# Stick-breaking attention inside a hybrid decoder step: narrow tiles' sums a beat earlier, exponentials behind the newest split, masked weights split a beat later

## The chip, the cores and the metric

The kernel runs on one core of a Trainium2 chip. The time is the device time of one execution in microseconds (us). Engines are TensorE (PE in the profile; PEld is its weight load), VectorE (DVE), ScalarE (ACT), GpSimd (POOL) and SyncE (SP), which issues almost all DMAs here.

## The reference

One layer of a decoder step: an input projection of 1,072 tokens (16 learned, 1,024 of a prompt, 8 x 4 new ones of samples), eight heads of stick-breaking attention beside four heads of gated linear attention, SiLU gates and an output projection. The change lies in the attention of the prompt:

```python
def stick_break_weights(z, mask):
    sp = jnp.where(mask, jax.nn.softplus(z), 0.0)
    later = lax.cumsum(sp, axis=z.ndim - 1, reverse=True) - sp
    return jnp.where(mask, jnp.exp(jax.nn.log_sigmoid(z) - later), 0.0)

a = stick_break_weights(sb_logits(qb, k, bias), kpos[None, :] < qpos[:, None])
o = jnp.einsum('bhqk,bkhd->bqhd', a.astype(v.dtype), v)
```

A key's weight is its own sigmoid, times what all later keys have left of the stick: softplus of the logits is summed over the later keys, and the exponential of logit minus sum is the weight.

## The kernel before, in words

All float32 products are made from an upper part (rounded to the matmul's format) and a lower part (the rest), three matmuls for each product of two split operands. Attention runs in the stage from about 100 to 860 us. The main stream on TensorE is the in-projection (`inproj`, L347 to L349): head by head the columns of v, k and q, each as 16 steps of 128 rows in three chunks of tokens. After every six of these matmuls the program calls `W.beat()`. At a beat a small scheduler (`Weaver`) resumes generators, each of which writes some instructions and yields a number of beats to wait. So the order on every engine is laid down in beats, and each engine then works in that order; an engine that waits for an operand holds back all that stands behind it.

Per head there are 14 tiles (qi, j): query block qi (0: queries 16 to 527; 1: 528 to 1039) against a group j of 126 keys, from the last key group down. Keys lie on the partitions, queries on the columns. Query block 1 has tiles j = 8 to 0, block 0 j = 4 to 0. A tile that is cut by the causal border has fewer columns: 32, 158, 284 and 410 for (1,8) to (1,5), 24, 150, 276 and 402 for (0,4) to (0,1), and about 512 elsewhere. One tile (`attend_tile`) goes through these steps:

- z = k^T q, three matmuls (L599 to L601) into a PSUM bank `z`.
- X = softplus(z + bias): VectorE's minimum (L605), ScalarE's exponential and logarithm (L606, L607), VectorE's maximum (L608); GpSimd clears what lies above the border (L611).
- Two beats later, and when the next key group's tile has its sums: ScalarE copies that tile's total into row 0 of X (the carry, L617), and X is split: `hi_s` by ScalarE (L584), `lo_s` by VectorE (L585).
- D1 = 4 beats later the sums: two matmuls with a triangular matrix, `hi_s` and `lo_s`, onto z (L620, L621). z is now logit minus sum.
- Y = exp(z + bias) on ScalarE (L625), the border cleared by GpSimd (L627), Y split into `hi_a` and `lo_a` by the same function `split_tmp`.
- D2 = 6 beats later the product with V into `O`, three matmuls (L633 to L635).

Upper parts share three buffers (tag `hi`), lower parts three (`lo`), X and Y three. ScalarE also splits the k columns of the next head (L703), the weights (`wh_q`, `wh_v`, L187) and V (`V`, L576). V of a head is not taken from the projection directly: `load_v` clears a staging tile `vr` on GpSimd (L571), loads the head's values into it from the output tensor that they were stored to (DMAs L572 and L574), and splits it (L576 on ScalarE, L578 on VectorE), in three pieces.

Three more generators run beside this: `z_feed` (the decode samples' logits on VectorE, L469, from page loads `kp`, L426, and query copies `qb`, L446), `weight_forms` (differences of the output weights, L496), and `level_masks` (seven masks for the gated linear attention, built on GpSimd from a cleared tile by pairs of selections, L404 to L408). `spread(ins)` and the note "behind" add a dependency that only orders: the instruction is placed later than another (for `spread`, the newest in-projection matmul, `W.mark`) in the program's order, and no semaphore is added for it.

Of the kernel before, what the change touches and what calls it, by code (L numbers as in the profile page):

```python
# [15 lines left out]
AF = mybir.ActivationFunctionType  # L16
ALU = mybir.AluOpType
# [37 lines left out]
NOSYNC = mybir.DependencyInfo(mybir.DependencyClass.NoSync, mybir.DependencyReason.DATA)  # L55
# [34 lines left out]
def hybrid_step(ctx: ExitStack, tc: tile.TileContext, x_prompt, x_sample, cache_k, cache_v, state_gla,  # L90
# [5 lines left out]
    vec, act, pool = nc.vector, nc.scalar, nc.gpsimd  # L96
# [19 lines left out]
    def stage(nm, dt=F32):  # L116
        return stg.tile([P, 384], dt, tag="stg", name=nm)
# [77 lines left out]
    with tc.tile_pool(name="xp", bufs=2) as xp, tc.tile_pool(name="xps", bufs=5, space=PSUM) as xps:  # L195
# [109 lines left out]
        for c, (lo, hi) in enumerate(XCHUNKS):  # L305
            n = hi - lo
            for k in range(NK):
# [10 lines left out]
                ins = act.activation(hh[k][:, lo:hi], ps[:, :n], AF.Copy, scale=gpre[:, k:k + 1]).ins  # L318
# [79 lines left out]
    def level_masks():  # L398

        for m in (64, 32, 16, 8, 4, 2, 1):  # L400
            nb = P // (2 * m)
            a = stage(f"lv{m}")[:, :P]
            av = a.rearrange("p (n two m) -> p n two m", two=2, m=m)
            pool.memset(a, 1.0)  # L404
            for two, k0 in ((1, 0), (0, m)):
                pool.affine_select(av[:, :, two, :], av[:, :, two, :], [[-2 * m, nb], [0, m]], ALU.is_ge, 0.0,
                                   base=-k0, channel_multiplier=1)
                pool.affine_select(av[:, :, two, :], av[:, :, two, :], [[2 * m, nb], [0, m]], ALU.is_ge, 0.0,  # L408
                                   base=k0 + m - 1, channel_multiplier=-1)
            lvl[m] = dk.tile([P, P], U8, tag=f"lvl{m}", bufs=1, name=f"lvl{m}")  # L410
            vec.tensor_copy(lvl[m][:], a)
            yield 16
# [66 lines left out]
    def spread(ins):  # L479

        if W.mark is not None:
            tc.add_manual_dep(ins.ins, W.mark.name, NOSYNC, reason="spread")
# [54 lines left out]
    with tc.tile_pool(name="sp", bufs=1) as sp, tc.tile_pool(name="sps", bufs=1, space=PSUM) as sps:  # L537
# [26 lines left out]
        def load_v(h, V, behind):  # L564

            for c in range(3):
                st = stage(f"vr{h}_{c}")
                sv = st[:].rearrange("p (a d) -> p a d", d=P)
                nt = 3 if c < 2 else 2
                src = new_v_prompt[0, 0, :, h, :]  # L570
                pool.memset(st[:], 0.0)  # L571
                nc.sync.dma_start(sv[1:KT + 1, :nt], src[c * 378:c * 378 + nt * KT].rearrange("(a p) d -> p a d", p=KT))  # L572
                if c == 2:
                    nc.sync.dma_start(sv[1:33, 2, :], src[8 * KT:REAL])  # L574
                vs = slice(3 * c, 3 * c + 3)
                ins = act.copy(V[0][:, vs, :], sv)  # L576
                tc.add_manual_dep(ins.ins, behind.name, NOSYNC, reason="behind")
                vec.tensor_tensor(V[1][:, vs, :], sv, V[0][:, vs, :].bitcast(F32), ALU.subtract)  # L578
                yield 1

        def split_tmp(X, rows, n, nm):
            a = sp.tile([P, 512], F32R, tag="hi", bufs=3, name=f"hi_{nm}")
            b = sp.tile([P, 512], F32R, tag="lo", bufs=3, name=f"lo_{nm}")
            act.copy(a[:rows, :n], X)  # L584
            vec.tensor_tensor(b[:rows, :n], X, a[:rows, :n].bitcast(F32), ALU.subtract)  # L585
            return a, b

        def attend_tile(h, qi, qlo, qhi, j, jmax, q, kt, V, carry, O):
            nm = f"{h}_{qi}_{j}"
            k0 = j * KT  # L590
            nk = P
            c0 = max(qlo, k0)
            col = c0 - qlo
            n = qhi - c0
            qs = slice(c0 - META, c0 - META + n)
            ks = slice(j * P, j * P + nk)
            z = sps.tile([P, 512], F32, tag="z", bufs=4, name=f"z{nm}")
            zz = z[:nk, :n]
            mm(zz, kt[0][:, ks], q[0][:, qs], start=True, stop=False)  # L599
            mm(zz, kt[0][:, ks], q[1][:, qs], start=False, stop=False)  # L600
            mm(zz, kt[1][:, ks], q[0][:, qs], start=False, stop=True)  # L601
            bias = bias0[:nk, h:h + 1]
            xt = sp.tile([P, 512], F32, tag="X", bufs=3, name=f"X{nm}")
            X = xt[:nk, :n]
            vec.tensor_scalar(X, zz, bias, 30.0, ALU.add, ALU.min)  # L605
            act.activation(X, X, AF.Exp)  # L606
            act.activation(X, X, AF.Ln, bias=1.0)  # L607
            vec.scalar_tensor_tensor(X, zz, bias, X, ALU.add, ALU.max)  # L608
            w = min(n, k0 + KT - c0)
            if w > 0:  # L610
                pool.affine_select(X[:, :w], X[:, :w], [[1, w]], ALU.is_gt, 0.0, base=c0 - k0 + 1, channel_multiplier=-1)  # L611
            yield 2
            if j < jmax:
                while carry.get(qi, (None,))[0] != j + 1:
                    yield 1
                _, cz, ccol = carry[qi]
                act.activation(X[0:1, ccol - col:], cz[0:1, :], AF.Copy, scale=-1.0)  # L617
            sh, sl = split_tmp(X, nk, n, "s" + nm)
            yield D1
            mm(zz, ntri0[:nk, :nk], sh[:nk, :n], start=False, stop=False, skip_group_check=True)  # L620
            mm(zz, ntri0[:nk, :nk], sl[:nk, :n], start=False, stop=True, skip_group_check=True)  # L621
            carry[qi] = (j, zz, col)
            yt = sp.tile([P, 512], F32, tag="X", bufs=3, name=f"Y{nm}")
            Y = yt[:nk, :n]
            act.activation(Y, zz, AF.Exp, bias=bias)  # L625
            if w > 0:
                pool.affine_select(Y[:, :w], Y[:, :w], [[1, w]], ALU.is_gt, 0.0, base=c0 - k0 + 1, channel_multiplier=-1)  # L627
            ah, al = split_tmp(Y, nk, n, "a" + nm)
            yield D2
            if j == jmax:  # L630
                O[qi] = sps.tile([P, 512], F32, tag="O", name=f"O{h}_{qi}")
            o = O[qi]
            mm(o[:, col:], V[0][:nk, j, :], ah[:nk, :n], start=(j == jmax), stop=False, skip_group_check=True)  # L633
            mm(o[:, col:], V[0][:nk, j, :], al[:nk, :n], start=False, stop=False, skip_group_check=True)
            mm(o[:, col:], V[1][:nk, j, :], ah[:nk, :n], start=False, stop=(j == 0), skip_group_check=True)  # L635
            if j == 0:
                st = sp.tile([P, 512], F32, tag="X", bufs=3, name=f"ost{h}_{qi}")
                act.copy(st[:], o[:])
                nc.sync.dma_start(od[h][:, qlo - META:qhi - META], st[:])
# [10 lines left out]
        D1, D2 = 4, 6  # L650
# [83 lines left out]
        W.spawn(z_feed(lambda n: 2), lasting=True)  # L734
        W.spawn(weight_forms(), 10, lasting=True)
        W.spawn(level_masks(), 30, lasting=True)
        for h in range(HEADS):
            if h == HEADS - 1:
# [977 lines left out]
```

## Time and profile before

| | us |
|---|---|
| median of three runs | 2051.52 (2050.90 to 2051.88) |
| profiled execution | 2053.43, span 2051.7 |
| granted TensorE clock, mean | 0.999 |
| TensorE busy | 2014.6 (98%) |
| VectorE busy | 1548.0 (75%) |
| ScalarE busy | 954.4 (47%) |
| GpSimd busy | 91.8 (4%) |

The profiled execution is one run under the hardware profiler; its own time stands beside the span of its records. Busy times are sums over the instructions of an engine. Timelines give an instruction's start, its length, its line, and, in brackets, how long the engine was idle before it and what ended that. Matmuls are pipelined, so that the lengths of two neighbours overlap; the distance between their starts is what a matmul costs.

### The profile page before, as it was taken

To read this page: it belongs to the slowest core of one execution; us is meant where nothing else is said; L and a number is where in the kernel's file an instruction comes from. 1 tells how busy PE (TensorE), PEld (TensorE's weight loads), DVE (VectorE), ACT (ScalarE), POOL (GpSimd) and SP (SyncE) were. 2 spreads that over 40 slices of the span, in tenths; PEclk is the share of its full clock that TensorE was granted. 3 is DMA by queue.
4 is the path that set the end of the run, shared out by engine and by line. 5 is a ranking of instruction groups with operands and counts; after the bars stand their busy time and mean duration, and the time that the engine had idled before them with its cause. 6 is when DMAs were issued, how large, how long until landed. Compare 5 with 4: busy or idle time off the path is not lost.

```text
span 2051.7 us, 41912 instructions
## 1 busy us (share of the span) xinstructions
PE 2014.6 (98%) x12443; PEld 1857.7 (91%) x12443; DVE 1548.0 (75%) x6282; ACT 954.4 (47%) x2297; POOL 91.8 (4%) x338
## 2 busy tenths in 40 slices
PE   6999999999999999999999999999999999999998
PEld 5999999999999998999999999999888897788776
DVE  7368989888988989999798898978444347453576
ACT  7355556564655556432534335353433325432342
POOL 0012000101000000100000000000000000000000
PEclk9999999999999999999999999999999999999999
DMA  6355454644555542443342433335767666352475
GB/s 203 100 137 151 143 155 135 170 132 143 150 164 145 141 129 76 130 114 84 98 117 78 127 83 108 101 88 166 247 226 236 215 227 195 131 164 73 138 266 200
DMA packets 371821, 301.85 MB, mean 147 GB/s; under 512 B 42360, under 2 KB 312104, under 8 KB 371592
## 3 DMA queue, kind: packets, MB, share of 16 engines
q1 hardware_dynamic: 371288, 298.64, 48.7%
q8 instruction: 98, 1.61, 0.3%
q14 instruction: 131, 1.07, 0.2%
q10 hardware_dynamic: 304, 0.53, 0.1%
HBM read 241.75 MB, written 57.31 MB: 146 GB/s over the span
## 4 chain that ended last, share of the span: by engine, by line
PE 80%; DVE 8%; DMA 5%; issue 3%; ACT 3%; SPq 1%; POOL 0%; DVEq 0%; ACTq 0%; POOLq 0%
PE acc_g L347 5%; PE acc_g L348 5%; PE acc_g L349 5%; PE b L1617 4%; PE b L1619 4%; PE b L1618 4%; PE acc_k L347 3%; PE acc_k L349 3%; PE acc_k L348 3%; PE acc_gv L347 3%; DVE jk L469 3%; PE acc_gv L348 3%; PE acc_gv L349 3%; PE acc_v L347 2%; PE acc_q L347 2%
## 5 line engine op out<-in xcount | busy, mean ns | idle before, releaser
L469 DVE SCALAR_TENSOR_TENSOR jk<-kp,qb 128x128 f32<-128x128 f32 x2048 | 594.7, 290 | 43.7 <-DMA qb<-qsd 1.7
L347 PE MATMUL acc_g<-hT,wh_g 128*128 128x368 f32 (+2 forms) x768 | 251.0, 327 | 0.0
L349 PE MATMUL acc_g<-hT,wl_g 128*128 128x368 f32 (+2 forms) x768 | 246.8, 321 | 1.4 <-DVE wl_g L190 1.4
L348 PE MATMUL acc_g<-hT,wh_g 128*128 128x368 f32 (+2 forms) x768 | 247.0, 322 | 0.0
L469 DVE DVE_READ_ACCUMULATOR jk<-kp,qb 128x1 f32 x2048 | 168.8, 82 | 0.0
L1617 PE MATMUL b<-ring,f 128*128 128x512 f32 x416 | 164.1, 394 | 2.9 <-DVE u L1486 1.3
L1618 PE MATMUL b<-ring,f 128*128 128x512 f32 x416 | 162.5, 391 | 0.2 <-DVE ring L1416 0.2
L1619 PE MATMUL b<-ring,f 128*128 128x512 f32 x416 | 162.0, 389 | 0.0
L347 PEld LDWEIGHTS acc_g<-hT,wh_g 128*128 128x128 f32 x768 | 144.3, 188 | 12.0 <-issue 10.7
L1416 DVE TENSOR_TENSOR ring<-wr,ring 128x512 fp32r<-128x512 f32 x104 | 71.3, 690 | 102.5 <-ACT ring L1415 100.3
L349 PEld LDWEIGHTS acc_g<-hT,wl_g 128*128 128x128 f32 x768 | 144.3, 188 | 1.7 <-DVE wl_g L190 1.7
L348 PEld LDWEIGHTS acc_g<-hT,wh_g 128*128 128x128 f32 x768 | 144.4, 188 | 0.7
L1415 ACT CAST ring<-wr 128x512 fp32r<-128x512 f32 x104 | 64.3, 621 | 145.4 <-PE b L1619 87.9
L347 PE MATMUL acc_gv<-hT,wh_gv 128*128 128x402 f32 (+2 forms) x384 | 130.3, 339 | 0.0
L347 PE MATMUL acc_k<-hT,wh_k 128*128 128x384 f32 (+1 forms) x384 | 126.3, 329 | 0.0
L348 PE MATMUL acc_gv<-hT,wh_gv 128*128 128x402 f32 (+2 forms) x384 | 125.3, 326 | 0.0
L349 PE MATMUL acc_gv<-hT,wl_gv 128*128 128x402 f32 (+2 forms) x384 | 125.0, 326 | 0.0
L347 PE MATMUL acc_q<-hT,wh_q 128*128 128x368 f32 (+2 forms) x384 | 124.9, 325 | 0.0
L349 PE MATMUL acc_k<-hT,wl_k 128*128 128x384 f32 (+1 forms) x384 | 124.6, 324 | 0.0
L348 PE MATMUL acc_k<-hT,wh_k 128*128 128x384 f32 (+1 forms) x384 | 124.4, 324 | 0.0
L349 PE MATMUL acc_q<-hT,wl_q 128*128 128x368 f32 (+2 forms) x384 | 123.3, 321 | 0.0
L348 PE MATMUL acc_q<-hT,wh_q 128*128 128x368 f32 (+2 forms) x384 | 123.2, 321 | 0.0
(466 smaller groups left out, 5282.0 us busy)
## 6 DMA issues: line engine op xcount, KB each, us to landing
kp<-in_cache_k_dram SPq DMA_DIRECT2D x512, 64.0 KB
vr<-in_cache_v_dram SPq DMA_DIRECT2D x64, 512.0 KB
qb<-qsd SPq DMA_DIRECT2D x64, 256.0 KB
wr_g<-in_w_in_dram SPq DMA_DIRECT2D x64, 256.0 KB
wr<-td SPq DMA_DIRECT2D x56, 256.0 KB
tf<-in_w_out_dram SPq DMA_DIRECT2D x48, 256.0 KB
td<-tf SPq DMA_DIRECT2D x48, 256.0 KB
wr<-in_w_out_dram SPq DMA_DIRECT2D x48, 256.0 KB
```

Of the source, the lines that this page charges most:

```text
L347: mm(acc[c][:, :n], wh, hh[k][:, lo:hi], start=(k == 0), stop=False)
L348: mm(acc[c][:, :n], wh, hl[k][:, lo:hi], start=False, stop=False)
L349: W.mark = mm(acc[c][:, :n], wl, hh[k][:, lo:hi], start=False, stop=(k == NK - 1)).ins
L469: ins = vec.scalar_tensor_tensor(jk[:], kp[:], 1.0, qbs[h, b][:, t, :], ALU.mult, ALU.mult, accum_out=zt[:, t, NPG - 1 - i:NPG - i])
L1415: act.copy(wh, r)
L1416: vec.tensor_tensor(wl, r, wh.bitcast(F32), ALU.subtract)
L1617: mm(bk[:], ah, wh, start=first and k == 0, stop=False, skip_group_check=True)
L1618: mm(bk[:], ah, wl, start=False, stop=False, skip_group_check=True)
L1619: mm(bk[:], al, wh, start=False, stop=last and k == 7, skip_group_check=True)
```

## The change

It makes five edits, all of them to the order in which work is issued; no instruction of TensorE, VectorE or ScalarE is added or removed.

1. `level_masks`: the clearing and the selections on GpSimd are placed behind the newest in-projection matmul, and two beats pass between the pairs.
2. `load_v`: the clearing of `vr` is placed behind the newest in-projection matmul, and the loads into it come behind it.
3. The exponential of X (L606) is placed behind the newest `hi_s` on ScalarE.
4. The sums of tiles of up to 300 columns come three beats behind their split, instead of four.
5. Tiles with a causal border wait a beat between the mask of Y and the split of Y, and a beat less before the product with V.

```diff
--- before.py
+++ after.py
@@ -401,12 +401,13 @@
             nb = P // (2 * m)
             a = stage(f"lv{m}")[:, :P]
             av = a.rearrange("p (n two m) -> p n two m", two=2, m=m)
-            pool.memset(a, 1.0)
+            spread(pool.memset(a, 1.0))
             for two, k0 in ((1, 0), (0, m)):
-                pool.affine_select(av[:, :, two, :], av[:, :, two, :], [[-2 * m, nb], [0, m]], ALU.is_ge, 0.0,
-                                   base=-k0, channel_multiplier=1)
-                pool.affine_select(av[:, :, two, :], av[:, :, two, :], [[2 * m, nb], [0, m]], ALU.is_ge, 0.0,
-                                   base=k0 + m - 1, channel_multiplier=-1)
+                spread(pool.affine_select(av[:, :, two, :], av[:, :, two, :], [[-2 * m, nb], [0, m]], ALU.is_ge, 0.0,
+                                          base=-k0, channel_multiplier=1))
+                spread(pool.affine_select(av[:, :, two, :], av[:, :, two, :], [[2 * m, nb], [0, m]], ALU.is_ge, 0.0,
+                                          base=k0 + m - 1, channel_multiplier=-1))
+                yield 2
             lvl[m] = dk.tile([P, P], U8, tag=f"lvl{m}", bufs=1, name=f"lvl{m}")
             vec.tensor_copy(lvl[m][:], a)
             yield 16
@@ -568,7 +569,7 @@
                 sv = st[:].rearrange("p (a d) -> p a d", d=P)
                 nt = 3 if c < 2 else 2
                 src = new_v_prompt[0, 0, :, h, :]
-                pool.memset(st[:], 0.0)
+                spread(pool.memset(st[:], 0.0))
                 nc.sync.dma_start(sv[1:KT + 1, :nt], src[c * 378:c * 378 + nt * KT].rearrange("(a p) d -> p a d", p=KT))
                 if c == 2:
                     nc.sync.dma_start(sv[1:33, 2, :], src[8 * KT:REAL])
@@ -581,9 +582,13 @@
         def split_tmp(X, rows, n, nm):
             a = sp.tile([P, 512], F32R, tag="hi", bufs=3, name=f"hi_{nm}")
             b = sp.tile([P, 512], F32R, tag="lo", bufs=3, name=f"lo_{nm}")
-            act.copy(a[:rows, :n], X)
+            ins = act.copy(a[:rows, :n], X)
+            if nm[0] == "s":
+                newest_s[:] = [ins.ins]
             vec.tensor_tensor(b[:rows, :n], X, a[:rows, :n].bitcast(F32), ALU.subtract)
             return a, b
+
+        newest_s = []
 
         def attend_tile(h, qi, qlo, qhi, j, jmax, q, kt, V, carry, O):
             nm = f"{h}_{qi}_{j}"
@@ -603,7 +608,9 @@
             xt = sp.tile([P, 512], F32, tag="X", bufs=3, name=f"X{nm}")
             X = xt[:nk, :n]
             vec.tensor_scalar(X, zz, bias, 30.0, ALU.add, ALU.min)
-            act.activation(X, X, AF.Exp)
+            ins = act.activation(X, X, AF.Exp)
+            if newest_s:
+                tc.add_manual_dep(ins.ins, newest_s[0].name, NOSYNC, reason="behind")
             act.activation(X, X, AF.Ln, bias=1.0)
             vec.scalar_tensor_tensor(X, zz, bias, X, ALU.add, ALU.max)
             w = min(n, k0 + KT - c0)
@@ -616,7 +623,7 @@
                 _, cz, ccol = carry[qi]
                 act.activation(X[0:1, ccol - col:], cz[0:1, :], AF.Copy, scale=-1.0)
             sh, sl = split_tmp(X, nk, n, "s" + nm)
-            yield D1
+            yield D1 if n > 300 else D1 - 1
             mm(zz, ntri0[:nk, :nk], sh[:nk, :n], start=False, stop=False, skip_group_check=True)
             mm(zz, ntri0[:nk, :nk], sl[:nk, :n], start=False, stop=True, skip_group_check=True)
             carry[qi] = (j, zz, col)
@@ -625,8 +632,10 @@
             act.activation(Y, zz, AF.Exp, bias=bias)
             if w > 0:
                 pool.affine_select(Y[:, :w], Y[:, :w], [[1, w]], ALU.is_gt, 0.0, base=c0 - k0 + 1, channel_multiplier=-1)
+            if w > 0:
+                yield 1
             ah, al = split_tmp(Y, nk, n, "a" + nm)
-            yield D2
+            yield D2 - (w > 0)
             if j == jmax:
                 O[qi] = sps.tile([P, 512], F32, tag="O", name=f"O{h}_{qi}")
             o = O[qi]
```

In the listings below a name like `X2_0_1` is X of head 2, tile (0,1); in the changed kernel the lines are higher by one to nine.

ScalarE in head 2, between tiles (0,2) and (0,1), while the k of head 3 is split. Before:

```order
L606 ACTIVATE X2_0_0_6167<-X2_0_0_6167 128x512
L555 COPY st_k3_2_6180<-tk_k3_2_6179 128x256
L607 ACTIVATE X2_0_0_6167<-X2_0_0_6167 128x512
L556 COPY st_k3_2_6180<-tk_k3_2_6179 48x128
L625 ACTIVATE Y2_0_2_6191<-z2_0_2_5928,bias0_827 128x276
L617 ACTIVATE X2_0_1_6063<-z2_0_2_5928 1x276
L584 CAST hi_a2_0_2_6194<-Y2_0_2_6191 128x276
L584 CAST hi_s2_0_1_6199<-X2_0_1_6063 128x402
L625 ACTIVATE Y2_0_1_6279<-z2_0_1_6059,bias0_827 128x402
L617 ACTIVATE X2_0_0_6167<-z2_0_1_6059 1x402
```

Now:

```order
L611 ACTIVATE X2_0_1_6077<-X2_0_1_6077 128x402
L614 ACTIVATE X2_0_1_6077<-X2_0_1_6077 128x402
L632 ACTIVATE Y2_0_2_6101<-z2_0_2_5938,bias0_827 128x276
L624 ACTIVATE X2_0_1_6077<-z2_0_2_5938 1x276
L585 CAST hi_s2_0_1_6124<-X2_0_1_6077 128x402
L554 COPY st_k3_0_6135<-tk_k3_0_6134 128x384
L585 CAST hi_a2_0_2_6141<-Y2_0_2_6101 128x276
L554 COPY st_k3_1_6152<-tk_k3_1_6151 128x384
```

The upper part of X (0,1) came behind the k splits, the exponential of X (0,0), Y (0,2) and the upper part of Y (0,2); now it stands directly behind Y (0,2) and the carry, and the upper part of Y behind it.

GpSimd in head 0, around the mask of Y (0,2). Before (`k0_1`, `k1_1` are head 1's keys, `vr1` its V staging):

```order
L404 MEMSET lv2_2861 128x128
L571 MEMSET vr1_0_3077 128x384
L406 AFFINE_SELECT lv2_2861<-lv2_2861 128x32x2 x2
L571 MEMSET vr1_1_3109 128x384
L408 AFFINE_SELECT lv2_2861<-lv2_2861 128x32x2 x2
L571 MEMSET vr1_2_3149 128x384
L627 AFFINE_SELECT Y0_0_2_2685<-Y0_0_2_2685 128x126
```

Now:

```order
L618 AFFINE_SELECT X0_0_2_2424<-X0_0_2_2424 128x126
L634 AFFINE_SELECT Y0_0_3_2507<-Y0_0_3_2507 128x126
L634 AFFINE_SELECT Y0_0_2_2586<-Y0_0_2_2586 128x126
L618 AFFINE_SELECT X0_0_1_2561<-X0_0_1_2561 128x126
L700 MEMSET k0_1_1886 128x8x2
L701 MEMSET k0_1_1886 128x128
L700 MEMSET k1_1_1887 128x8x2
```

The level mask `lv2` and the three clearings of `vr1` no longer stand ahead of the mask of Y (0,2); the mask is followed by that of X (0,1) and then by the clearing of the next head's keys.

ScalarE at the start of head 1, around the splits of V. Before:

```order
L725 ACTIVATE q0_1_2514<-acc_q1_2_2519 128x272
L576 CAST V0_1_3060<-vr1_0_3077 128x384
L576 CAST V0_1_3060<-vr1_1_3109 128x384
L576 CAST V0_1_3060<-vr1_2_3149 128x384
L728 ACTIVATE qsm1_2516<-acc_q1_2_2519 128x32
L606 ACTIVATE X1_1_8_3118<-X1_1_8_3118 128x32
L663 COPY qtok1_3163<-qst1_3161 32x128
L607 ACTIVATE X1_1_8_3118<-X1_1_8_3118 128x32
L668 COPY zns1_3168<-zn1_3166 32x32
L584 CAST hi_s1_1_8_3172<-X1_1_8_3118 128x32
```

Now:

```order
L611 ACTIVATE X1_1_8_3110<-X1_1_8_3110 128x32
L614 ACTIVATE X1_1_8_3110<-X1_1_8_3110 128x32
L577 CAST V0_1_3052<-vr1_0_3069 128x384
L585 CAST hi_s1_1_8_3164<-X1_1_8_3110 128x32
L672 COPY qtok1_3155<-qst1_3153 32x128
L677 COPY zns1_3160<-zn1_3158 32x32
L577 CAST V0_1_3052<-vr1_1_3101 128x384
L611 ACTIVATE X1_1_7_3172<-X1_1_7_3172 128x158
L614 ACTIVATE X1_1_7_3172<-X1_1_7_3172 128x158
L577 CAST V0_1_3052<-vr1_2_3141 128x384
L187 CAST wh_v2_2_3370<-wr_v2_2_3368 128x512
L632 ACTIVATE Y1_1_8_3224<-z1_1_8_3106,bias0_827 128x32
```

The three splits of V stood together behind the last copy of q; now they stand apart, between the steps of tiles (1,8) and (1,7), with the first two ahead of the exponential of (1,7) and the third ahead of a weight split, Y (1,8) and the carry of (1,7).

## Rows read from the trace of the kernel before

**Rows 1.** Page, part 1: engine, busy us, share, instructions
```profile
PE 2014.6 (98%) x12443; PEld 1857.7 (91%) x12443; DVE 1548.0 (75%) x6282; ACT 954.4 (47%) x2297; POOL 91.8 (4%) x338
```

**Rows 2.** Windows, attention stage: us, busy (x) by engine, PEclk, DMA, GB/s
```profile
100.00:860.00 760.00, 756.01 (x4631) 724.96 (x4631) 667.48 (x3034) 430.89 (x1035) 73.63 (x254) 1.00 0.50 140
```

**Rows 3.** Waits, PE: waited for: us in total, times, longest
```profile
PE z L621 <- DVE lo_s L585: 2.3, 8, 0.8
PE z L620 <- ACT hi_s L584: 1.4, 3, 0.9
```

**Rows 4.** Waits, PE's weight loader (PEld), columns as before
```profile
PEld z L621 <- DVE lo_s L585: 5.8, 12, 1.1
PEld z L620 <- ACT hi_s L584: 3.3, 6, 1.2
```

**Rows 5.** Timeline, PE, head 1: start, length, operation xcount [idle before <-releaser]
```profile
232.15 0.34 PE L349 MATMUL acc_v<-hT,wl_v 128*128 128x384 f32 x1
232.33 0.35 PE L620 MATMUL z<-hi_s,ntri 128*128 128x410 f32 x1
232.52 0.40 PE L621 MATMUL z<-lo_s,ntri 128*128 128x410 f32 x1
```

**Rows 6.** Timeline, PE, head 0, sums of (0,1)
```profile
191.00 0.32 PE L349 MATMUL acc_q<-hT,wl_q 128*128 128x368 f32 x1
192.25 0.45 PE L620 MATMUL z<-hi_s,ntri 128*128 128x402 f32 x1 [0.93 <-ACT hi_s L584]
192.87 0.45 PE L621 MATMUL z<-lo_s,ntri 128*128 128x402 f32 x1 [0.17 <-DVE lo_s L585]
```

**Rows 7.** Timeline, PE, first and last of the places
```profile
138.40 0.45 PE L620 MATMUL z<-hi_s,ntri 128*128 128x410 f32 x1 [0.18 <-ACT hi_s L584]
...
838.22 0.45 PE L621 MATMUL z<-lo_s,ntri 128*128 128x402 f32 x1
```

**Rows 8.** Timeline, PE, head 4, sums of (1,5)
```profile
510.72 0.45 PE L620 MATMUL z<-hi_s,ntri 128*128 128x410 f32 x1 [0.26 <-ACT hi_s L584]
511.40 0.46 PE L621 MATMUL z<-lo_s,ntri 128*128 128x410 f32 x1 [0.22 <-DVE lo_s L585]
```

**Rows 9.** Timeline, ACT, head 2, tiles (0,2) and (0,1)
```profile
374.87 0.49 ACT L625 ACTIVATE Y<-z,bias 128x276 f32<-128x276 f32 x1
...
375.81 0.42 ACT L584 CAST hi_a<-Y 128x276 fp32r<-128x276 f32 x1 [0.18 <-POOL Y L627]
376.14 0.52 ACT L584 CAST hi_s<-X 128x402 fp32r<-128x402 f32 x1
```

**Rows 10.** Timelines, POOL, then ACT, head 0, tile (0,2)
```profile
188.11 1.45 POOL L406 TENSOR_SCALAR_AFFINE_SELECT lv<-lv 128x64 f32<-128x64 f32 x2
...
189.87 0.83 POOL L408 TENSOR_SCALAR_AFFINE_SELECT lv<-lv 128x64 f32<-128x64 f32 x2
...
191.35 0.42 ACT L584 CAST hi_a<-Y 128x276 fp32r<-128x276 f32 x1 [1.46 <-POOL Y L627]
```

**Rows 11.** Chain that ended last (start, us, what), then timeline, ACT, head 4
```profile
487.98 4.85 DMA vr<-out_dram
...
492.86 0.52 ACT L576 CAST V<-vr 128x384 fp32r<-128x384 f32 x1 [2.04 <-DMA vr<-out_dram]
```

**Rows 12.** Timelines, SP's issues, then PE, head 1
```profile
211.16 0.34 SPq L426 DMA_DIRECT2D kp<-in_cache_k_dram  x1
211.61 0.39 SPq L185 DMA_DIRECT2D wr_v<-in_w_in_dram  x1
...
218.04 0.18 PE L620 MATMUL z<-hi_s,ntri 128*128 128x32 f32 x1
```

**Rows 13.** Timelines, SP's issue, then ACT, head 5
```profile
579.08 0.41 SPq L574 DMA_DIRECT2D vr<-out_dram  x1
...
580.77 1.46 ACT L576 CAST V<-vr 128x384 fp32r<-128x384 f32 x3
```

**Rows 14.** Chain that ended last, head 0: start, us, what
```profile
120.63 5.98 DMA qb<-qsd
```

## The prediction

> **What bounds the kernel now.** I read the page's share of the span first: TensorE is busy 98% of it [rows 1], so only matmuls taken away, or waits ahead of matmuls, can change the time. The order listings show that no matmul is added or removed and that the order on TensorE differs in the attention stage alone, about 100 to 860 us, where the eight heads run beside the in-projection. There the windows give TensorE 756.0 of 760 us, VectorE 667.5 (88%), ScalarE 430.9 [rows 2]: the whole stake is a few microseconds of TensorE waiting.
>
> The waits by engine say for what. TensorE stands 2.3 us in eight waits ahead of L621 for a lower part `lo_s`, and 1.4 us in three ahead of L620 for an upper part `hi_s` [rows 3]. Its weight loader, which has to load for the same matmuls, stands 5.8 us in 12 and 3.3 us in six [rows 4]. These are the sums over the triangular matrix, two matmuls per tile. The first view (3.7 us) is too low, since the end of a matmul is modelled and overlaps the next; the second (9.1 us) is too high, since a loader normally waits a little anyway. So I go by distances between starts. Undisturbed, L620 starts 0.18 us after the matmul ahead of it and L621 0.19 us after L620 [rows 5]. In head 0, tile (0,1), the distances are 1.25 and 0.62 us [rows 6]: 1.1 and 0.4 us lost. Worked out at all 18 loader waits of rows 4 in that way (the first is the pair at 138.40, the last the one at 838.22 [rows 7]) the loss is **7.6 us**: 5.0 in tile (0,1) of the eight heads, 0.85 in tile (1,5) of head 0, 1.64 in tiles (1,6) and (1,5) of head 4 (510.72 to 511.40, 0.68 instead of 0.19, is one of its four sums [rows 8]), 0.1 in head 7. It lies between the two views, and whatever goes of it shortens the span one for one.
>
> Why the operands are late is read from ScalarE and GpSimd. Tile (0,1) needs the carry of (0,2). In head 2 the exponential of Y (L625) starts only at 374.87, because the splits of k and the next tile's exponential stand ahead of it in ScalarE's order. Then ScalarE waits for GpSimd's mask of Y before `hi_a`, and `hi_s`, which the sums want, comes behind that at 376.14 [rows 9]. In head 0 it is worse: GpSimd spends 1.45 and 0.83 us on pairs of level masks, and `hi_a` waits 1.46 us for the mask of Y, with `hi_s` behind it [rows 10]. In head 4 a V load took 4.85 us to land, and ScalarE's V cast waited 2.04 us for it, with everything behind [rows 11].
>
> **The change part by part**, against the profiled execution of 2053.43 us (span 2051.7, 1.7 outside it), which lies 1.9 above the median of 2051.52.
>
> Exponentials behind the newest split, and the masked split of Y one beat later: by the order listing ScalarE now has Y (0,2), carry, `hi_s` (0,1), and only then `hi_a`, the k splits and the next exponential. `hi_s` no longer stands behind GpSimd or the k splits. This removes the 5.0 us of the (0,1) tiles. What it delays is `hi_a` and the next tile's X; the product with V stays six beats behind the sums, and an X has its own beats before it is split, so I cost the delay at nothing while VectorE keeps up (rival B otherwise).
>
> Level masks and the clearing of the V staging tile pinned behind the last in-projection matmul: in head 0 the 1.45 and 0.83 us pairs go away from the masks of Y. That is part of the same 5.0. Splitting the pairs adds rows on GpSimd and no work.
>
> Sums of tiles of up to 300 columns a beat earlier: a beat is six in-projection matmuls, about 1.1 us at 0.18 a start [rows 5]. It takes margin away (lower and upper part must be ready a beat sooner) and gives margin to the next tile, whose carry comes earlier. It also shifts the order so that an upper part's buffer is free sooner. The 0.85 and 1.64 us of (1,5) and (1,6) I count as removed: both trace back to a chain that now starts earlier. Their bounds are 0 and 2.5 us; I take all because the wide tiles keep their four beats.
>
> So far −7.6. Two new waits stand against it.
>
> *V loads.* They are now issued at the q in-projection's end: by SyncE's order, head 1's first stands directly ahead of the weight load that went out at 211.61, 0.45 us after the issue before it [rows 12], and the others behind; before, all had gone out by then. The V casts stand on ScalarE between the exponential and the split of tile (1,8), (1,7) and on VectorE ahead of `lo_s` and the next X. The (1,8) sums, which stood at 218.04 [rows 12], come some nine matmuls earlier, near 216.5. Working back over the cast (0.52 [rows 11]) and some 0.4 for the splits of 32 columns, the first load must have landed by about 215.6, within about 4.4 us of its issue. In head 5 a load issued at 579.08 was there when its cast came, the last of three that began at 580.77 and took 1.46 together, so within 2.6 us [rows 13]; at that price the term is zero. At the 4.85 us of rows 11 it is some 0.4 us a head, 3.1 in eight. I take 1.5, halfway, since heads differ in what else is in flight.
> The Trainium skill's page "DMA: Bandwidth & Descriptors" (section "Latency and other measured facts") says that the round trip to HBM dominates a fixed cost of about 2 us and grows from 0.2 to 2 us under load. By its light case the term would be zero and the time 2045.3; the 4.85 us row is longer than that fixed cost even so, and the measurement decides; 2045.3 is the lower end of my forecast below, no case of its own.
>
> *The first z-feed product in head 0* waits for `qb`, whose load took 5.98 us [rows 14]. The chain runs through that load already; what now follows the product on VectorE includes lower parts that are due one to three beats sooner. Bounds 0 and 1.7 us (the 5.98 less the four beats of about 1.08 that a wide tile keeps); I take 1.4, nearer the upper end because the wait itself is certain.
>
> Sum: 2051.52 − 7.6 + 1.5 + 1.4 = **2046.8 us** (2048.7 for an execution like the profiled one).
>
> **The rivals.**
> A, slower: *late V loads stall every head as in head 4*. There one late landing cost 1.64 us. Eight such heads cost 13.1; less the 7.6 that goes, the time is 2057.0. It decides where loads land later than those 4.4 us after their issue; for it speaks rows 11, against it rows 13, and that head 4's wait held up more behind it than one cast.
> B, half stays: *VectorE becomes what the sums wait for.* It is 88% busy in the stage, in order, with a beat less for narrow tiles; already most loader waits are for `lo_s` [rows 4]. If half of the 7.6 stays beside my 2.9 of new waits: 2050.6.
> C, clean: both new waits are hidden: 2043.9, which is the most that can be had.
> D, *the order-only hints move nothing that is late*: 2051.5. The order listing speaks against it, since `hi_s` does move ahead.
>
> **How the numbers follow.** What this kernel's measurement can tell from no change is about 0.2%, 4.1 us, so faster means below 2047.4. My forecast (new waits between 1.4 and 4.5 us, 2045.3 to 2048.4) gets 0.45, C 0.17, B 0.25, D 0.03, A 0.10. Of the forecast about 0.7 lies below 2047.4, with C that makes 0.49 faster; B, D and the rest make 0.41 within; A makes 0.10 slower. The range leaves out A and the lowest part of C: 2044.2 to 2052.0.
>
> **What would show it.** In the profile after, waits for `lo_s` and `hi_s` ahead of the sums should fall from 9.1 us at the loader to about 3, with none left in tile (0,1). `hi_s` of (0,1) should start ahead of the k splits, and the level masks should not stand next to a mask of Y. The late V loads should show as waits of the V cast for `vr` in some heads, not in all, and `qb` as VectorE's wait in head 0. I am wrong if the sums still wait 6 us or more (B), or if V casts wait in nearly all heads and sums (1,8) to (1,6) with them (A), or if TensorE loses time at a place where it lost none before: at a first product with q, say, for want of a buffer that the later `hi_a` holds.

## The result and the profile after

| | us | runs | granted clock |
|---|---|---|---|
| before, median | 2052.27 (2049.10 to 2054.55) | 8 | 0.999 (profiled) |
| changed, median | 2058.47 (2055.43 to 2061.94) | 8 | 0.996 to 0.998 |

The ratio is 1.0029, 95% interval [1.0020, 1.0038]: 6.2 us slower, where 4.7 us less was forecast. The changed kernel's profiled execution, 2055.43 us with a span of 2053.6, is the fastest of its eight; a second one, below, took 2058.37.

The waits that the prediction wanted gone are mostly gone. The loader's waits in the changed kernel (L627 and L628 are the sums now, L585 and L588 the splits):

```profile
PEld z L628 <- DVE lo_s L588: 3.4, 4, 1.6
PEld z L627 <- ACT hi_s L585: 0.8, 1, 0.8
```

That is 4.2 us in five waits against 9.1 in 18 [rows 4]. Tile (0,1) is no longer among them. ScalarE in head 2 answers to rows 9: `hi_s` of 402 columns starts 1.27 us after Y (0,2) as before, but Y is there early, and `hi_a` stands behind:

```profile
365.68 0.47 ACT L632 ACTIVATE Y<-z,bias 128x276 f32<-128x276 f32 x1
366.47 0.39 ACT L624 ACTIVATE X<-z 1x276 f32<-1x276 f32 x1 [0.32 <-DVE X L615]
366.95 0.53 ACT L585 CAST hi_s<-X 128x402 fp32r<-128x402 f32 x1
...
367.76 0.42 ACT L585 CAST hi_a<-Y 128x276 fp32r<-128x276 f32 x1
```

What came instead is seen on ScalarE and VectorE. By the waits, V casts now stand for their loads 12 times, in all eight heads, where the prediction said in some; before it was once, the 2.04 us of rows 11. VectorE stands behind them, for the V casts:

```profile
ACT V L577 <- DMA vr<-out_dram: 12.1, 12, 3.9
...
DVE V L579 <- ACT V L577: 9.5, 8, 3.7
```

Head 4 is the worst. Its timelines show SyncE's issues, then ScalarE, VectorE and TensorE, and last the windows around it (us, busy and count of PE, PEld, DVE, ACT, POOL, the granted clock, DMA share, GB/s):

```profile
485.50 2.51 SPq L573 DMA_DIRECT2D vr<-out_dram  x3
...
490.85 1.17 ACT L577 CAST V<-vr 128x384 fp32r<-128x384 f32 x2 [3.85 <-DMA vr<-out_dram]
...
491.39 1.22 DVE L579 TENSOR_TENSOR V<-vr,V 128x384 fp32r<-128x384 f32 x2 [3.69 <-ACT V L577]
...
495.73 0.32 DVE L588 TENSOR_TENSOR lo_s<-X,hi_s 128x158 fp32r<-128x158 f32 x1
...
494.27 0.34 PE L627 MATMUL z<-hi_s,ntri 128*128 128x158 f32 x1 [0.52 <-ACT hi_s L585]
496.10 0.34 PE L628 MATMUL z<-lo_s,ntri 128*128 128x158 f32 x1 [1.49 <-DVE lo_s L588]
...
497.42 0.52 PE L349 MATMUL acc_v<-hT,wl_v 128*128 128x384 f32 x1
497.74 0.54 PE L604 MATMUL z<-q,k 128*128 128x410 f32 x1
...
488.00:492.00 4.00, 4.00 (x29) 4.00 (x27) 0.56 (x1) 1.00 (x3) 0.00 (x0) 1.00 0.50 114
492.00:496.00 4.00, 2.09 (x13) 1.62 (x11) 3.85 (x17) 2.59 (x10) 0.59 (x2) 1.00 0.11 30
496.00:500.00 4.00, 3.90 (x15) 3.87 (x16) 3.86 (x22) 1.79 (x6) 0.59 (x2) 0.61 0.35 98
500.00:504.00 4.00, 4.00 (x26) 4.00 (x26) 4.00 (x15) 2.86 (x6) 0.59 (x2) 0.96 0.46 100
```

The three loads go out in 2.51 us; ScalarE stands 3.85 us for the first, with X (1,7) behind it, and VectorE 3.69. The sums of (1,7) then wait 0.52 and 1.49 us. And that is not all: from about 497 to 500 us TensorE is granted 1.2 GHz instead of 2.4 (0.61 and 0.96 are means over four microseconds), and the 384 columns that take 0.17 us a start elsewhere take 0.32. At clocks of 0.61 and 0.96, 0.39 and 0.04 of 4 us are lost, 1.7 us. Nothing like it stands in the attention stage of before, where the clock is 1.00 throughout [rows 2].

A smaller loss shows in head 7, at the sums of (0,4), where the profile of before has no wait:

```profile
819.73 0.17 PE L627 MATMUL z<-hi_s,ntri 128*128 128x24 f32 x1
820.85 0.28 PE L628 MATMUL z<-lo_s,ntri 128*128 128x24 f32 x1 [0.95 <-DVE lo_s L588]
...
819.39 0.68 DVE L588 TENSOR_TENSOR lo_a<-Y,hi_a 128x512 fp32r<-128x512 f32 x1
820.01 0.47 DVE L519 SCALAR_TENSOR_TENSOR gs<-gx,gs 128x304 f32<-128x304 f32 x1
...
820.62 0.18 DVE L588 TENSOR_TENSOR lo_s<-X,hi_s 128x24 fp32r<-128x24 f32 x1
```

VectorE is full of gate work (`gs`) there, and `lo_s`, 0.18 us long, has its turn at 820.62; TensorE wanted it at 819.8. In the run without edits 2 and 4 below, where these sums come a beat later, TensorE does not wait there.

How long the attention stage takes can be read apart from the rest: the first 500 of the 12,443 matmuls and those from the 5,200th on come in the same order in every kernel of this document. From the start of the 500th (at about 99 us) to that of the 5,200th (at about 870 us) the profile of before takes 771.15 us, and this one of the changed kernel 770.33. So in this execution, the fastest of eight, gains and losses of the stage cancel, and what it is behind arose later, where 1181.4 us have become 1184.7; a stretch at half the clock, at 1736 to 1740 us, is in it. That last part takes between 1179.1 and 1185.0 us in all profiles here, in kernels that are faster than before as well, so a single profile cannot tell a loss of 3 us there from scatter.

### The profile page after: what moved, and what is told of

It is laid out like the page before. It is cut to its first block, busy times and chain, and to the rows that moved or that the text cites. A ratio compares the mean times of both kernels' runs of the same rounds, so it can differ in the third digit from the quotient of the medians.

```text
span 2053.6 us, 41951 instructions
## 1 busy us (share of the span) xinstructions
PE 2016.2 (98%) x12443; PEld 1861.0 (91%) x12443; DVE 1544.8 (75%) x6282; ACT 958.3 (47%) x2297; POOL 91.6 (4%) x338
## 4 chain that ended last, share of the span: by engine, by line
PE 80%; DVE 9%; DMA 6%; ACT 2%; issue 2%; SPq 1%; DVEq 0%; POOL 0%; ACTq 0%; POOLq 0%
PE acc_g L347 5%; PE acc_g L348 5%; PE acc_g L349 5%; PE b L1626 4%; PE b L1628 4%; PE b L1627 4%; DVE jk L470 3%; PE acc_k L347 3%; PE acc_k L349 3%; PE acc_k L348 3%; PE acc_q L347 3%; PE acc_q L348 3%; PE acc_q L349 3%; PE acc_gv L347 3%; PE acc_gv L348 3%; PE acc_gv L349 3%
```

## The experiments

Times are compared as the ratio to runs of the kernel before on the same chip, since that kernel itself moves by a few microseconds between chips; 0.1% is 2.05 us. The last column is the time from the 500th to the 5,200th matmul in the one profile of each kernel (the changed kernel has two); before has 771.15 us.

| kernel | median us | before, same chip | ratio | 95% interval | stage in the profile, us |
|---|---|---|---|---|---|
| changed, edits 1 to 5 | 2058.47 | 2052.27 | 1.0029 | 1.0020 to 1.0038 | 770.33, 773.69 |
| without 2 | 2053.42 | 2054.11 | 0.9993 | 0.9984 to 1.0002 | 769.88 |
| without 2 and 4 | 2047.86 | 2053.48 | 0.9974 | 0.9962 to 0.9986 | 766.16 |
| without 2; 4 in heads 1 to 6 only | 2050.86 | 2054.70 | 0.9986 | 0.9977 to 0.9994 | 766.33 |
| 1 alone | 2054.77 | 2054.70 | 1.0000 | 0.9992 to 1.0009 | 769.40 |
| 2 alone | 2061.09 | 2054.11 | 1.0032 | 1.0020 to 1.0044 | 778.26 |
| 3 alone | 2052.45 | 2054.70 | 0.9991 | 0.9982 to 1.0000 | 771.53 |
| 4 alone | 2055.34 | 2054.11 | 1.0006 | 0.9996 to 1.0015 | 771.31 |
| 5 alone | 2049.73 | 2054.70 | 0.9973 | 0.9963 to 0.9983 | 765.71 |
| 4 and 5 | 2054.40 | 2054.70 | 0.9998 | 0.9990 to 1.0007 | 768.17 |
| 2 and 5 | 2053.64 | 2054.70 | 0.9994 | 0.9986 to 1.0003 | 772.36 |
| changed, V splits later | 2055.96 | 2053.48 | 1.0009 | 1.0000 to 1.0018 | 770.90 |
| without 2, V splits later | 2051.26 | 2053.48 | 0.9989 | 0.9980 to 0.9998 | 766.62 |
| without 2 and 4, V splits later | 2047.59 | 2053.48 | 0.9970 | 0.9958 to 0.9982 | 764.79 |
| 5, V splits later | 2047.99 | 2054.70 | 0.9961 | 0.9949 to 0.9973 | 766.35 |

### First: which edit costs

Theory V blames the late V loads, theory S the earlier sums, theory L something behind the attention stage.

Without the second edit:

```diff
-                spread(pool.memset(st[:], 0.0))
+                pool.memset(st[:], 0.0)
```

> The changed kernel without its second edit: the staging tile of V is cleared and loaded as early as before; all else as changed, and TensorE's order is that of the changed kernel. Theory V (the V loads, issued late, land after their casts' turn; TensorE then waits at the sums of (1,8) to (1,6) and is granted half the clock for a while behind a long wait): 2044 to 2047.5 us, no clock below 1.00 in head 4, no V cast that waits for vr, waits for lo_s and hi_s at the loader under 2 us. Theory S (the narrow tiles' sums, a beat earlier, are what is too early): 2056 to 2060, as the changed kernel. Theory L (the time is lost behind the attention stage, where the order is the same in both): about 2055 to 2058, ahead of before at 860 us and behind it at the end.

The second edit alone is the same line the other way, on the kernel before.

> The kernel before with the second edit alone: V cleared and loaded late. Theory V: 2055 to 2061 us, with V casts that wait for vr, and TensorE waiting at (1,8) to (1,6) in some heads. Theory S: 2051 to 2053, since the sums keep their four beats and cover the later load.

The fourth edit alone:

```diff
-            yield D1
+            yield D1 if n > 300 else D1 - 1
```

> The kernel before with the fourth edit alone: sums of tiles of up to 300 columns three beats behind their split. Theory S: 2055 to 2060 us, with more and longer waits for lo_s than the 5.8 us of before. Theory V: 2050 to 2053.

And the changed kernel once more:

> The changed kernel once more, for a second profile, since its runs spread over 6 us and the one profile shows the fastest of them. Theory V: V casts wait for vr in one to five heads, not in the same ones each time, and each wait of TensorE over 1.5 us is followed by a stretch at half the clock; 2055 to 2062 us. Theory L: the loss lies behind 860 us.

The second edit costs 0.36% in company (1.0029 against 0.9993) and 0.32% alone, 6.6 to 7.4 us. This much of theory V holds. With the edit alone V casts wait 17.2 us for their loads, and the loader's waits ahead of the sums are 16.4 us instead of 9.1:

```profile
ACT V L576 <- DMA vr<-out_dram: 17.2, 12, 3.0
...
PEld z L621 <- DVE lo_s L585: 11.8, 22, 1.4
PEld z L620 <- ACT hi_s L584: 4.6, 7, 1.3
```

The difference of 7.3 us there is about the whole loss, and the stage takes 7.1 us more than before (778.26 against 771.15); this profile has no stretch at half the clock. But "without 2" missed its expectation: 2053.42, not 2044 to 2047.5, and three V casts still wait for `vr`, 4.2 us in all. In head 0 its V loads are not as early as before: three of the four go out at 116.0 to 117.1 us, where before has all four out by 102, and with the first edit alone they go out as late. So this run leaves a part of the late loads in. Theory S is right in part as well, only the fourth edit alone does not show it: its 2055.34 us lie where the theory put them, but the kernel before took 2054.11 there (0.06%, interval on both sides of none). Its profile tells why. With the fourth edit alone the waits at (0,1), 402 columns, become waits at the next tile, (0,0), 512 columns; head 0:

```profile
191.86 0.34 PE L349 MATMUL acc_q<-hT,wl_q 128*128 128x384 f32 x1
192.88 0.49 PE L620 MATMUL z<-hi_s,ntri 128*128 128x512 f32 x1 [0.68 <-ACT hi_s L584]
193.60 0.50 PE L621 MATMUL z<-lo_s,ntri 128*128 128x512 f32 x1 [0.23 <-DVE lo_s L585]
```

The second profile of the changed kernel shows the long wait of head 4 in the same place as the first, the sums of (1,7), 1.49 us again, and one more in head 0, both with the same sequel. V casts there wait 14.3 us in 13, in all eight heads, where one to five had been expected. ScalarE and SyncE, then TensorE and VectorE in head 0, TensorE in head 4, and the windows in both:

```profile
121.21 0.51 ACT L577 CAST V<-vr 128x384 fp32r<-128x384 f32 x1 [2.25 <-DMA vr<-out_dram]
121.63 0.17 ACT L677 COPY zns<-zn 32x32 f32<-32x32 f32 x1
...
121.83 0.31 SPq L678 DMA_DIRECT2D znd<-zns  x1
122.70 0.93 SPq L447 DMA_DIRECT2D qb<-qsd  x2
...
129.71 0.38 PE L627 MATMUL z<-hi_s,ntri 128*128 128x284 f32 x1
131.67 0.40 PE L628 MATMUL z<-lo_s,ntri 128*128 128x284 f32 x1 [1.58 <-DVE lo_s L588]
...
129.13 0.29 DVE L470 SCALAR_TENSOR_TENSOR jk<-kp,qb 128x128 f32<-128x128 f32 x1 [2.27 <-DMA qb<-qsd]
...
131.16 0.45 DVE L588 TENSOR_TENSOR lo_s<-X,hi_s 128x284 fp32r<-128x284 f32 x1
...
499.80 0.34 PE L628 MATMUL z<-lo_s,ntri 128*128 128x158 f32 x1 [1.49 <-DVE lo_s L588]
...
128.00:132.00 4.00, 2.42 (x17) 2.21 (x16) 2.77 (x16) 0.62 (x1) 0.00 (x0) 1.00 0.41 109
132.00:136.00 4.00, 4.00 (x17) 3.71 (x16) 4.00 (x15) 2.56 (x6) 0.58 (x2) 0.58 0.25 67
496.00:500.00 4.00, 2.51 (x16) 2.07 (x14) 3.91 (x20) 2.58 (x9) 0.58 (x2) 1.00 0.18 46
500.00:504.00 4.00, 4.00 (x18) 3.98 (x18) 3.86 (x22) 2.11 (x6) 0.59 (x2) 0.66 0.33 92
```

The head 0 wait is the one for `qb` that the prediction named: VectorE stands 2.27 us for it, and the `lo_s` that TensorE wants has its turn at 131.16, behind the products that were held up. But `qb` itself is late with the V loads. Its load goes out at 122.70, behind the store of `zns` in SyncE's order, and `zns` is copied on ScalarE behind the V cast that waited 2.25 us. In the first profile, where that cast waited 0.15 us, the store goes out at 119.38 and `qb` at 120.42, and TensorE does not wait at (1,6). In the eight kernels with all V loads of head 0 out by 102 us, `qb` goes out between 120.20 and 120.95.

Each stretch at half the clock costs some 1.7 us (42% of 4 us) on top of the wait. A third lies at 952 to 960 us, behind a wait of 1.93 us for another stage's operand, where the order is as before; the same wait, of 0.6 to 1.9 us in other profiles, was not followed by one. Nor was one of 1.79 us at 1742.9 in this profile, so the expectation that each wait over 1.5 us has this sequel fails. The granted clock of the runs fits such stretches in the changed kernel: its mean is 0.9970 over eight runs, against 0.9984 over the eleven without the second edit. The difference, 0.0014 of 2054 us, is 2.9 us, an estimate of the clock's part in the 7.4. With the second edit alone it is 0.998 in all six runs, against 0.9982 before, so that there the price is waiting.

Theory L does not explain the price of the second edit, since the profile with that edit alone shows it within the stage, and kernels with the same later part are 0.26% below the kernel before. The two profiles of the changed kernel do not refute it by themselves: the first shows no loss within the stage, and the second, 4.9 us longer than that of before, has half of this there (773.69 us) and half behind it.

### Second: the place of the V splits, and the beat

The three splits of V are written some beats behind their loads:

```diff
+            svs = []
             for c in range(3):
...
+                svs.append(sv)
+            yield 5
+            for c, sv in enumerate(svs):
                 vs = slice(3 * c, 3 * c + 3)
                 ins = act.copy(V[0][:, vs, :], sv)
-                tc.add_manual_dep(ins.ins, behind.name, NOSYNC, reason="behind")
+                spread(ins)
```

With late loads (and `yield 8`):

> The changed kernel, V loads late as in it, but the three splits of V written eight beats behind the loads, so that on ScalarE and VectorE they stand behind the steps of tiles (1,8) and (1,7) and not among them. Theory V (the splits' place, not the late load as such, is what costs): no V cast waits for vr over 0.5 us, waits at the sums of (1,8) to (1,6) under 1 us in all, 2049 to 2053 us where the kernel before has 2051 to 2054, so 5 to 9 us less than the changed kernel. Rival (the late loads cost by their traffic, or by what they hold up on SyncE): 2056 to 2060, as the changed kernel.

With early loads:

> The changed kernel without its second edit, and the splits of V five beats behind the loads. Theory V: the two waits of TensorE for qsm (1.05 and 1.28 us in heads 1 and 5 of the run without the second edit, where V casts stand ahead of qsm) go, 1.5 to 2.5 us below that run, 0.1 to 0.2% below the kernel before. Rival (waits only move to the next place): no difference from the run without the second edit.

Without the second and fourth edit (both lines above undone), and the same with the splits later:

> The changed kernel without its second and fourth edit: V early, all sums four beats behind their split. Theory W (a beat less leaves VectorE no margin): the waits for lo_s at (1,6) of head 0 (0.9 us) and (0,4) of head 7 (1.1 us) of the run without the second edit go, 1 to 3 us below that run. Rival (the earlier sums are what frees the upper parts' buffers and starts the wide tiles sooner): waits at (1,5) of head 0 and (1,6), (1,5) of head 4 come back as before, 0 to 3 us above that run.

> As the run before it, with the splits of V five beats behind the loads. Theories V and W together: the lowest of the four, 2046 to 2050 us against 2051 to 2054 of the kernel before (0.15 to 0.3% less). If waits only move: as the kernel before.

Moving the splits behind late loads takes 0.2% off the changed kernel: V casts wait 1.1 us, not 12.1, and no sum of (1,8) to (1,6) waits. So about half of the second edit's price lies in the splits' place. The forecast of 2049 to 2053 was missed: with early loads and late splits the ratio is 0.9989, another 0.2% less. The profile shows one place for it, head 0, where TensorE waits for V itself, before a product with V. TensorE, then VectorE:

```profile
129.40 0.26 PE L647 MATMUL O<-lo_a,V 128*128 128x32 f32 x1
132.58 0.28 PE L648 MATMUL O<-hi_a,V 128*128 128x32 f32 x1 [2.92 <-DVE V L583]
...
128.22 0.29 DVE L470 SCALAR_TENSOR_TENSOR jk<-kp,qb 128x128 f32<-128x128 f32 x1 [3.23 <-DMA qb<-qsd]
...
131.97 0.55 DVE L583 TENSOR_TENSOR V<-vr,V 128x384 fp32r<-128x384 f32 x1
```

The last lower part of V has its turn at 131.97, behind 3.23 us of VectorE's wait for `qb`, whose load goes out at 122.48; with early loads and late splits it goes out at 120.44, VectorE waits 1.36 us and TensorE not at all. A stretch at half the clock follows here too (0.65 and 0.92 in the windows from 132 to 140 us). So the rival is right in part: the late loads also cost by what they hold up behind them on SyncE. How much of the 2.92 us is theirs and how much comes of eight beats in place of five is open, since late loads with five beats were not tried.

With early loads the later splits gave 0.04%, with the fourth edit (the waits for `qsm` gone) as without it, within the interval. The fourth edit is the larger item: taking it out as well gives 0.19%, with the splits in either place, and the kernel with edits 1, 3 and 5 is 0.26% below the kernel before. Waits at (1,5) of head 0 come back with it (0.58 and 0.48 us of loss), as the rival had it, but those of (1,6) and (1,5) in head 4 do not.

### Third: which of the three helps

> The kernel before with the fifth edit alone: masked weights split a beat later, so that on ScalarE the upper part of X (0,1) stands ahead of that of Y (0,2). Theory P (the place of hi_s behind hi_a and GpSimd's mask is what makes (0,1) late): the (0,1) waits fall from 5.0 to under 2 us, 0.1 to 0.2% below the kernel before. Rival (Y behind the k splits is the cause, which this edit does not move): no difference.

> The kernel before with the first edit alone: level masks spread on GpSimd. Theory P: only head 0's (0,1) gains, its 1.5 us at most: within 0.1% of the kernel before. Rival (GpSimd's masks hold up more heads than one): over 0.1% below it.

> The kernel before with the third edit alone: the exponential of X behind the newest upper part. At the (0,1) tiles it changes no place, so by theory P within 0.1% of the kernel before; it could gain only at (1,5) and (1,6) of heads 0 and 4, 2.5 us at most. Rival (this edit carries the gain of the three that help together, 5.4 us): 0.15% or more below it.

The fifth edit is the last hunk of the change:

```diff
+            if w > 0:
+                yield 1
             ah, al = split_tmp(Y, nk, n, "a" + nm)
-            yield D2
+            yield D2 - (w > 0)
```

The runs of the first and the third take their hunks as they stand. The fifth edit alone gives all of it, 0.27%, more than its theory asked for; the stage takes 765.71 us, 5.4 less than before. ScalarE in head 2 with it:

```profile
373.74 0.48 ACT L625 ACTIVATE Y<-z,bias 128x276 f32<-128x276 f32 x1
374.12 0.37 ACT L617 ACTIVATE X<-z 1x276 f32<-1x276 f32 x1
374.52 0.53 ACT L584 CAST hi_s<-X 128x402 fp32r<-128x402 f32 x1
374.96 0.42 ACT L584 CAST hi_a<-Y 128x276 fp32r<-128x276 f32 x1
```

Y (0,2) still stands behind the k splits; only `hi_s` and `hi_a` have changed places, so that `hi_s` starts 0.78 us after Y and not 1.27 [rows 9]. That was enough. In head 0 the matmul distances at (0,1) fall from 1.25 and 0.62 us [rows 6] to normal and 0.47. The first edit does nothing that can be measured; the third lies between nothing and 0.18%.

The fourth edit in heads 1 to 6 only, without the second:

```diff
-            yield D1 if n > 300 else D1 - 1
+            yield D1 - (n <= 300 and 0 < h < HEADS - 1)
```

> The changed kernel without its second edit, and with the fourth in heads 1 to 6 only. Theory W (a beat less costs where VectorE is short: in head 0, beside the wait for qb, and in head 7, beside the gates): 1.5 to 3 us below the run without the second edit, so 0.1 to 0.25% below the kernel before. Rival (the beat costs in every head): as the run without the second edit, 0.0 to 0.1% below.

It recovers 0.07% of the 0.19%, with intervals that overlap on both sides. Its profile puts more on heads 0 and 7: the stage takes 766.33 us, against 769.88 with the beat less in all heads and 766.16 with it in none. That these two heads bear part of the price is shown; how much, is not.

### Fourth: do the edits add up

> The kernel before with the fourth and fifth edits. Theory M (both take away the same waits, those of tile (0,1), and the fourth puts new ones in their place: lo_s of (0,0), qsm, (0,4) of head 7): little of the fifth edit's 0.27% is left, 0.05 to 0.15% below the kernel before, with the (0,4) wait of head 7 near 1.07 us. Rival (the fourth edit's cost in company comes from the third or first): 0.2 to 0.3% below.

> The kernel before with the second and fifth edits. Theory V: the late V loads cost what they cost alone (0.32%) and the fifth edit gains what it gains alone (0.27%): 0.0 to 0.15% above the kernel before, V casts waiting for vr 10 to 18 us in all. Rival (with hi_s ahead the sums have the margin to take the late loads): 0.1 to 0.25% below.

> The kernel before with the fifth edit, V loads early, the splits of V five beats behind the loads. Theory V: the waits for qsm in heads 1 and 5 (0.66 and 0.50 us with the fifth edit alone) go: 0.3 to 0.35% below the kernel before, the lowest of all. Rival (waits only move on): 0.25 to 0.28% below, as the fifth edit alone.

Edits 4 and 5 together are worth nothing: beside the fifth, the fourth costs 0.25%. Theory M holds, with less left over than it forecast. Both take away the waits of (0,1); what the fourth adds is its own, and 2.5 us of it show in the stage (768.17 against 765.71). The waits of TensorE with both:

```profile
PE acc_v L347 <- ACT qsm L730: 2.0, 2, 1.1
...
PE z L621 <- DVE lo_s L585: 1.0, 1, 1.0
```

The second row is (0,4) of head 7. The first is in heads 1 and 5, where the last V load comes late for its cast even with early loads, and `qsm`, behind that cast on ScalarE, frees the bank that the next in-projection wants; with the fifth edit alone the same two places lose 0.66 and 0.50 us. The second edit costs 0.21% beside the fifth (0.9994 against 0.9973), less than alone, so the pair came out 0.06% below the kernel before and not at or above it as expected. But V casts wait 16.1 us in 13 with it, as alone, and the stage is 6.6 us longer (772.36 against 765.71), nearly as alone; whether the fifth edit really takes part of the price away is open. The fifth edit with the V splits five beats later is the fastest kernel measured, 0.39% below the one before (2047.99 us against 2054.70 there). Against the fifth edit alone the intervals overlap, and the stage is no shorter in its profile (766.35 against 765.71); the `qsm` waits are gone, but a wait of 1.0 us for `lo_s` at (1,7) of head 1 has come.

## Why the prediction was wrong, point by point

**The removed term held for the most part, but not by the edits I gave it to.** I put 7.6 us of loss at the sums, 5.0 of it in (0,1). Without edits 2 and 4 the kernel gains 5.4 us (0.26%). I credited the exponentials' place, the earlier sums and the later split of Y together; the later split of Y does it alone. The 1.64 us of head 4, which I gave to the earlier sums, go without them too.

**"The chain now starts earlier", the fourth edit.** I wrote that it takes margin away, put no price on that in the sum, and counted 2.5 us for it. In company it costs 0.19 to 0.25%, 4 to 5 us. This is rival B's mechanism, which I priced as half of the 7.6 staying where it was; in fact most of the old places were cured and new ones came: (0,4) of head 7, longer waits for `qsm` in heads 1 and 5, and (0,0), most of all where the fifth edit is absent. No row of before shows a wait there, but the rows that show how full VectorE is [rows 2] were the hint.

**The V loads: the term that was mis-sized.** I took 1.5 us between 0 and 3.1, with one landing of 4.85 us as the upper end and a loss of 0.4 us per head. It cost 7.4 us in company. The bound was built from the sum's deadline, the first piece and a single landing. The wait begins when the cast has its turn on ScalarE: in head 1 that was 2.2 us after the issue, in head 4 1.5, where I had allowed 4.4 up to the sum. The second piece, which I left out, was waited for in seven heads of eight. The landing is no constant, and my 4.85 us were those of the last piece, of 16 KB: in head 4 of the changed kernel the chain has 5.48 us for a piece of 189 KB. The wait does not end at the cast: behind it, in order, stand X of the next tile on ScalarE and everything on VectorE, 12.1 and 9.5 us of waits for 24 pieces, and in head 0 `qb`. And a long wait of TensorE can be followed by half the clock, 1.7 us more. The chain's row:

```profile
486.01 5.48 DMA vr<-out_dram
```

The Trainium skill's page "DMA: Bandwidth & Descriptors" (section "Latency and other measured facts"), which I weighed as a possible reason for no cost at all, gives the access latency of HBM as 0.2 us on average and 2 us at high load, as the main part of a fixed cost of about 2 us. No run here parts the 5.48 us into latency, transfer and waiting behind other loads, so they neither bear that out nor speak against it.

**Rival A was the right side and nearly the right number.** It gave 2057.0 at a chance of 0.10; measured were 2058.47. Its mechanism, V casts waiting in line, is what happened: they wait in all eight heads, but TensorE loses much in one head or two, and not 1.64 us in each. That the number came so near is luck: its 13.1 us are nearly twice the 7.4 that the late loads cost, and the price of the earlier sums, which it did not have, makes up most of the rest. I argued against it with one early landing [rows 13] while rows 11 showed a late one and what it holds up. One row for and one against, on a load whose price is a whole chain, did not carry 0.10.

**`qb` in head 0.** The wait is there as I placed it, at (1,6): 1.58 us of TensorE in the second profile of the changed kernel, 0.9 us of loss without the second edit, none in the first profile. So my 1.4 had the right size in one profile of two. I had counted it as a term of its own, and it is in part the V loads' once more, which send `qb` out later. It was not tried by itself.

## What to carry to other kernels

Where an engine works in order, an instruction that waits for a transfer makes all behind it late, other loads included: here its place was about half of the price of a late load. Put it behind everything that somebody else waits for, or issue the load so early that it is sure to be there. When a late operand is cured by moving one instruction, test that move alone before adding others; here one edit of three lines held the whole gain, and two of the other four together gave back more than it. A margin in the order (here one beat) that no wait in the profile uses may still cover an engine that is 88% busy.

## What had not been expected of the hardware

The four longest waits of TensorE in the attention stage, 1.49 to 2.92 us (one of 1.49 behind another of 0.52), were each followed by a stretch of some 3.5 us at 1.2 GHz, in three profiles, and each such stretch cost some 1.7 us, about as much as most of the waits. The length of a wait alone does not decide it: in the stage behind, waits of 1.81 to 1.94 us for one operand were not followed by one in five other profiles. Also, in one profile of the changed kernel pieces of the same 189 KB landed about 2.6 us after their issue (head 1, 207.69 to 210.27) and 5.5 us after it (head 4), and the 16 KB piece of before within 2.6 us in head 5 [rows 13] and after 4.85 us in head 4 [rows 11].
